# The first feed-forward product as seven half products, in a two-layer encoder kernel on one core

## The chip, the cores and the metric

The kernel runs on one core of a Trainium2 chip, as one program. The metric is the device time in microseconds (us) of one execution. Beside the times there is one execution recorded by the hardware profiler, from which all durations of single instructions come. The engines are called PE (TensorE, the matrix engine), DVE (VectorE), ACT (ScalarE), POOL (GpSimd) and SP (SyncE, which here only starts DMA transfers). A matmul first loads 128 columns of weights (PEld in the profile) and then streams the other operand through them.

## What is computed

A trunk of two layers over 512 positions of width 1024, all in float32. Each layer has an attention part of two head groups, then a feed-forward part of width 4096; the output gets a last norm. Cut to what matters here:

```python
for l in range(DEPTH):                       # 2
    h = rmsnorm(x, attn_norm[l])
    proj = jnp.einsum('bsd,de->bse', h, w_in[l])
    ...                                      # stick-breaking and differential attention
    x = x + jnp.einsum('bse,ed->bsd', mixed, w_o[l])
    h = rmsnorm(x, mlp_norm[l])
    u = jnp.square(jax.nn.relu(jnp.einsum('bsd,df->bsf', h, w_ff1[l])))   # 512 x 1024 by 1024 x 4096
    x = x + jnp.einsum('bsf,fd->bsd', u, w_ff2[l])                        # 512 x 4096 by 4096 x 1024
return rmsnorm(x, final_norm)
```

## The kernel before

**Precision.** Each float32 operand is split into two float32r parts: a high part, rounded by ACT (`activation` with `Copy` into a float32r tile), and a low part, the rest, taken by DVE. A product is then three matmuls into one PSUM sum: high by high, high by low, low by high (`three`, L257 to L262). For weights the split is `split_part` (L102 on; ACT at L117, DVE at L118), for other operands `split` (L218 to L220).

**Weights.** All weight blocks are units of 128 x 1024 in the order of their use (`_UNITS`). `_Weights.next` hands out the next unit and first has the units up to three behind it split (one behind it in the attention part, where there are two places instead of four). Units that aren't of kind "f" stream through a ring of three raw tiles, loaded by SP (L100). After a unit has been split, functions kept for it in `then` run: they start further loads.

**The feed-forward part** (from L754 on) goes through four groups of 1024 of the 4096 inner columns, `GROUPS`, in each layer. Per group:

- First product: eight blocks of 128 inner columns (`block`, called in the loop over `k`). A block is eight chunks of `three` with the unit's 128 x 128 weights and 512 positions of h streamed, into one PSUM bank; the banks turn among five. The rms factor of h isn't applied here but later, to y, since relu and square let it through as its square (`r2`). `evict_u` (L776 on) applies relu (L787) and square (L788) on ACT, and for each pair of blocks makes the four quarters and four combinations of u that Strassen's scheme wants, 256 positions wide, and splits them.
- Second product, already by Strassen's algorithm (in Winograd's form): seven forms (`FORMS`), each of two units, with u's combinations as weights and 512 columns of w_ff2 combinations streamed, into two PSUM banks. `gather` adds each form's banks to its own y tile: ACT copies at the first group (L810), DVE adds later (L812).

The combinations of w_ff2 are made by DMA: `fetch` loads a quadrant by SP (L754), and `grow` adds another onto it by an accumulating DMA from POOL (L760), as soon as the form that needs the earlier contents has been split: "11" grows into "x1", then "x2", then "x4", and "21" into "x3". Their tiles are `kept`.

In the last group the seven y tiles are merged (`merge`: accumulating DMA between tiles; `join`: DVE), scaled by `r2` (`settle`), transposed back onto x (`back`) or, in the last layer, normed and written out (`square`, `root`, `weigh`, `store`).

**Around it.** Before it stands the second half of the output projection, `wo(0)`, which per 128 rows of the model width makes h (`make_h`, L223 and L224) and the running sum of squares (`add_sq`; POOL adds, L233). PSUM has eight banks: two "t" for transposes, two "mm", three "s", one "o". The cosine and sine tiles are reloaded (or, in the last layer, replaced by the final gains) in group 1.

**What sets the order.** Each engine and each DMA queue works its instructions in one order, fixed when the program is built by a planner that follows the order of the text and its own estimates of readiness.

## Time and profile before

| what | value |
|---|---|
| runs | 1160.62, 1161.37, 1165.87 us; median 1161.37 |
| profiled execution | 1164.68 us, span from first to last instruction 1162.8 us |
| granted TensorE clock | 0.995 |
| ACT busy | 656.1 us (56%) |
| POOL busy | 174.7 us (15%) |
| read from HBM | 138.17 MB, written 2.10 MB |

How to read it: "xN" is a count; in a group's row stand line, engine, operation, output from inputs, shape, count, then busy us, mean ns of one, and the engine's idle time just before these instructions with what ended it. Consecutive instructions of one engine overlap a little in the rows, so the cost of one more is read from the distance of two starts.

### The profile page before, as it was taken

The page shows a single profiled execution, that of the slowest core. Times are in us where ns is not written, and L with a number is a line of the kernel's source. Part 1 is how long each engine was busy: PE and PEld are TensorE (multiplying, and loading weights), DVE is VectorE, ACT ScalarE, POOL GpSimd, SP SyncE. Part 2 cuts the span into 40 slices and gives each one's busy share as a digit, 9 for nine tenths or more (in the row PEclk, how much of TensorE's full clock was granted, in tenths as well). Part 3 has the DMA queues.
Part 4 walks back from the last instruction along what each step waited for, and adds up shares of the span by engine and source line. Part 5 has one row for each costly group of instructions (what it writes and reads, how often), then busy time and mean ns, then how long its engine had stood idle before and what let it go on. Part 6 is the DMA issues. An engine that isn't in the chain of part 4 may idle for free.

```text
span 1162.8 us, 15712 instructions
## 1 busy us (share of the span) xinstructions
PE 1142.8 (98%) x5682; PEld 961.8 (83%) x5682; DVE 799.1 (69%) x1291; ACT 656.1 (56%) x1169; POOL 174.7 (15%) x243
## 2 busy tenths in 40 slices
PE   9999999999999999999899999999999999999996
PEld 7889888888888888888688898888888888888884
DVE  6898688765546656656869976877664466476567
ACT  6456666566656455364445566655666553553554
POOL 1001423130101101002000024322211010010022
PEclk9999999999999999999899999999999999999998
DMA  7564443255945836737416733622658367376185
GB/s 255 172 179 130 128 134 102 73 216 112 215 145 113 224 115 130 231 89 160 97 55 183 218 109 109 181 67 72 228 125 218 125 129 222 93 176 190 29 172 131
DMA packets 56861, 170.13 MB, mean 146 GB/s; under 512 B 7120, under 2 KB 8144, under 8 KB 56784
## 3 DMA queue, kind: packets, MB, share of 16 engines
q1 hardware_dynamic: 46416, 131.88, 35.3%
q0 software_dynamic: 10224, 37.23, 18.7%
q8 instruction: 45, 0.74, 0.3%
q14 instruction: 32, 0.26, 0.1%
q10 hardware_dynamic: 144, 0.02, 0.0%
HBM read 138.17 MB, written 2.10 MB: 121 GB/s over the span
## 4 chain that ended last, share of the span: by engine, by line
PE 88%; DVE 5%; DMA 2%; ACT 2%; issue 1%; POOL 1%; POOLq 0%; ACTq 0%; DVEq 0%
PE f L260 10%; PE f L261 10%; PE f L262 10%; PE x L261 4%; PE x L262 4%; PE x L260 4%; PE wo L260 3%; PE wo L261 3%; PE wo L262 3%; DVE wlo L118 1%; PE T1s L533 1%; PE T0s L533 1%; DMA q<-in_w 1%; DMA y<-y 1%; PE v0w L260 1%
## 5 line engine op out<-in xcount | busy, mean ns | idle before, releaser
L118 DVE TENSOR_TENSOR wlo<-raw,whi 128x1024 fp32r<-128x1024 f32 (+1 forms) x132 | 157.5, 1197 | 101.6 <-ACT whi L117 101.2
L118 DVE TENSOR_TENSOR wlo<-q,whi 128x512 fp32r<-128x512 f32 x224 | 145.9, 687 | 109.2 <-ACT whi L117 108.8
L117 ACT ACTIVATE whi<-raw 128x1024 fp32r<-128x1024 f32 (+1 forms) x132 | 134.0, 1020 | 118.1 <-PE f L261 55.3
L260 PE MATMUL f<-h_hi,whi 128*128 128x512 f32 x512 | 199.6, 390 | 0.0
L262 PE MATMUL f<-h_hi,wlo 128*128 128x512 f32 x512 | 199.3, 389 | 0.0
L261 PE MATMUL f<-h_lo,whi 128*128 128x512 f32 x512 | 199.2, 389 | 0.0
L117 ACT ACTIVATE whi<-q 128x512 fp32r<-128x512 f32 x224 | 129.5, 624 | 121.5 <-DMA q<-in_w 39.7
L760 POOL DMA_DIRECT2D q<-in_w x64 | 56.2, 884 | 557.4 <-DVE wlo L118 470.7
L262 PEld LDWEIGHTS f<-h_hi,wlo 128*128 128x128 f32 x512 | 96.1, 188 | 20.0
L260 PEld LDWEIGHTS f<-h_hi,whi 128*128 128x128 f32 x512 | 96.1, 188 | 19.9
L261 PEld LDWEIGHTS f<-h_lo,whi 128*128 128x128 f32 x512 | 96.1, 188 | 19.8
L220 DVE TENSOR_TENSOR Al<-F,Ah 128x256 fp32r<-128x256 f32 (+2 forms) x96 | 74.8, 779 | 44.1 <-ACT Ah L219 44.0
L260 PE MATMUL x<-whi,Ah 128*128 128x512 f32 x256 | 100.6, 393 | 0.0
L261 PE MATMUL x<-wlo,Ah 128*128 128x512 f32 x256 | 100.2, 391 | 0.2 <-DVE wlo L118 0.2
L262 PE MATMUL x<-whi,Al 128*128 128x512 f32 x256 | 100.2, 391 | 0.0
L219 ACT ACTIVATE Ah<-F 128x256 fp32r<-128x256 f32 (+2 forms) x96 | 67.6, 704 | 45.7 <-DVE F L796 43.8
L261 PEld LDWEIGHTS x<-wlo,Ah 128*128 128x128 f32 x256 | 48.2, 188 | 10.3 <-DVE wlo L118 0.5
L260 PEld LDWEIGHTS x<-whi,Ah 128*128 128x128 f32 x256 | 48.2, 188 | 10.2 <-ACT whi L117 0.5
L262 PEld LDWEIGHTS x<-whi,Al 128*128 128x128 f32 x256 | 48.3, 189 | 10.0
L787 ACT ACTIVATE F<-f 128x512 f32<-128x512 f32 x64 | 37.5, 587 | 10.9 <-DVE Al L220 5.5
L788 ACT ACTIVATE F<-F 128x512 f32<-128x512 f32 x64 | 40.3, 630 | 1.5
L223 ACT ACTIVATE h_hi<-x,g_all 128x512 fp32r<-128x512 f32 x32 | 22.6, 720 | 26.0 <-DVE x L664 13.0
(920 smaller groups left out, 2600.2 us busy)
## 6 DMA issues: line engine op xcount, KB each, us to landing
raw<-in_w SPq DMA_DIRECT2D x126, 512.0 KB, 3.5
q<-in_w SPq DMA_DIRECT2D x64, 512.0 KB, 5.5
q<-in_w POOLq DMA_DIRECT2D x64, 512.0 KB, 6.1
x<-in_xT SPq DMA_DIRECT2D x8, 256.0 KB, 4.3
raw<-in_w SPq DMA_DIRECT2D x8, 128.0 KB, 4.2
yx<-y POOLq DMA_DIRECT2D x2, 512.0 KB, 8.5
y<-y POOLq DMA_DIRECT2D x2, 512.0 KB, 7.6
y<-yx POOLq DMA_DIRECT2D x2, 512.0 KB, 6.0
```

What stands on the lines that cost most here:

```text
L117: h = nc.scalar.activation(hi[:, a:b], raw[:, a:b], AF.Copy)
L118: self.last = h, nc.vector.tensor_tensor(out=lo[:, a:b], in0=raw[:, a:b], in1=hi[:, a:b].bitcast(F32), op=ALU.subtract)
L219: nc.scalar.activation(hi, src, AF.Copy)
L220: nc.vector.tensor_tensor(out=lo, in0=src, in1=hi.bitcast(F32), op=ALU.subtract)
L223: a = nc.scalar.activation(h_hi[:, c, :], x[:, c, :], AF.Copy, scale=g)
L260: nc.tensor.matmul(pt, ah, bh, start=first, stop=False)
L261: nc.tensor.matmul(pt, ah, bl, start=False, stop=False)
L262: nc.tensor.matmul(pt, al, bh, start=False, stop=last)
L533: nc.tensor.transpose(pt[:, n * P : (n + 1) * P], u["w"][qi][:, kb * P : (kb + 1) * P], ident)
L760: nc.gpsimd.dma_start(t, quad(g, q, c), accum_op=ALU.add)
L787: nc.scalar.activation(t, pt, AF.Relu)
L788: nc.scalar.activation(t, t, AF.Square)
```

## The change

The first product also goes by Strassen's algorithm. h, as 1024 model rows by 512 positions, is cut into four quarters (rows 0 to 511 and 512 to 1023; positions 0 to 255 and 256 to 511), w_ff1 of the group likewise into quadrants by model rows and by inner columns. Seven half products (`HALVES`), each of two units, stream 256 positions instead of 512. Their results aren't kept apart: "1", then "6", "7" and "4" add onto one PSUM sum (a); "5" and then "3" onto a second (b); "2" has a third (c). Between these additions `tap` reads the running sums out. There are two of each sum, one per unit of a half product, so six banks hold sums.

- The combinations of h (`T_hi`, `T_lo`) are made at the start of each layer's feed-forward part (`opening`): x is scaled into `hx` by ACT, combined by DVE and split, four pieces of 1024 columns.
- The combinations of w_ff1 are made from quadrants in the array `w1`: `fill` loads them (for "x" with an accumulating DMA on top), `sum1` adds two tiles by DVE and, for "y", starts another accumulating DMA. w_ff1 leaves the raw ring.
- u: `F` holds five slots of 128 x 1024 for a whole group. `roll` splits one slot, 1024 wide, two forms ahead of its use; two places turn. Three of the combinations are made after form "11".
- Units of the second product are split in one piece of 1024 instead of two of 512.
- The tile pools are moved: the attention's temporary tiles lie on the right side and are closed before `wo(0)`, so that loads of the first group are started ahead of `wo(0)`; the squares in `wo(0)` get two slots (the cosine and sine tile) instead of four; the cosines, sines, gains and the next layer's first raw units are loaded in the last group (`tables`).

```diff
+HALVES = ("1", "2", "5", "6", "7", "4", "3")
+FSLOT = {"11": 1, "21": 3, "x1": 4, "22": 3, "x2": 1, "x3": 0, "x4": 2}
...
-            for f in range(2 * GP):
-                units.append(("1", l, g * 2 * GP + f))
+            for q in HALVES:
+                for c in range(GP // 2):
+                    units.append(("q", l, g, q, c))
...
-            else:
-                self.split_part(i, 0, 512)
-                self.split_part(i, 512, 1024)
+            self.split_part(i, 0, 1024)
...
-                            add_sq(db, db == 0, tt)
+                            add_sq(db, db == 0, lambda n: cs[:, db % 2, :])
...
+            def fill(what, g, c):
+                t = homes[(what, c)] if what in "yw" else kept["z.x".index(what)][c]
+                for q in {"y": "1", "z": "2", "x": "5", "w": "4"}[what] + {"y": "7", "x": "63"}.get(what, ""):
+                    W.raw[_AT[("q", l, g, q, c)]] = t
+                nc.sync.dma_start(t, quad1(g, {"y": "11", "z": "12", "x": "21", "w": "22"}[what], c))
+                if what == "x":
+                    nc.gpsimd.dma_start(t, quad1(g, "22", c), accum_op=ALU.add)
+
+            def sum1(what, g, c):
+                i = _AT[("q", l, g, "5", c)]
+                t, by = W.raw[i], W.raw[_AT[("q", l, g, "1" if what == "y" else "2", c)]]
+                nc.vector.tensor_add(t, t, by)
+                if what == "y":
+                    nc.gpsimd.dma_start(by, quad1(g, "21", c), accum_op=ALU.add)
...
+                    then("q", g, "5", c, sum1, "y", g, c)
+                    then("q", g, "6", c, sum1, "z", g, c)
+                    then("q", g, "6", c, fetch, g, "11", c)
+                    if g == 0:
+                        then("q", g, "7", c, fetch, g, "21", c)
+                    then("q", g, "3", c, fetch, g, "22", c)
...
+                    if g + 1 < GROUPS:
+                        then("q", g, "7", c, fill, "y", g + 1, c)
+                        then("q", g, "4", c, fill, "w", g + 1, c)
+                        then("f", g, "22", c, fill, "x", g + 1, c)
+                        then("f", g, "x3", c, fetch, g + 1, "21", c)
+                        then("f", g, "x4", c, fill, "z", g + 1, c)
+                    elif c:
+                        then("q", g, "4", c, tables)
+            for what in "yzx":
                 for c in range(GP // 2):
-                    fetch(0, form, c)
+                    fill(what, 0, c)
+
+            for _ in wo(0):
+                pass
...
+            def opening(n):
+                if n == 0:
+                    scaled(range(4))
+                    nc.vector.tensor_sub(hx[:, top, hi_t], hx[:, top, hi_t], hx[:, top, lo_t])
+                    t_part(top, hi_t)
+                    scaled(range(4, 8))
+                elif n == 1:
+                    nc.vector.tensor_sub(hx[:, bot, hi_t], hx[:, bot, lo_t], hx[:, bot, hi_t])
+                    nc.vector.tensor_sub(hx[:, top, lo_t], hx[:, bot, lo_t], hx[:, top, lo_t])
...
+                    t_part(bot, lo_t)
+                elif n == 2:
+                    t_part(top, lo_t)
+                    nc.vector.tensor_add(hx[:, bot, hi_t], hx[:, bot, hi_t], hx[:, top, hi_t])
+                    t_part(bot, hi_t)
...
+                if q == "1":
+                    nc.scalar.copy(f(1), pt)
+                elif q == "2":
+                    nc.vector.tensor_add(f(1), f(1), pt)
+                    bend(1)
+                elif q == "6":
+                    nc.scalar.copy(f(0), pt)
+                elif q == "7":
+                    nc.scalar.copy(f(2), pt)
+                    nc.vector.tensor_add(f(2), f(2), sums[("b", c)])
+                    bend(2, -1.0)
+                elif q == "4":
+                    bend(3, -1.0, pt)
+                elif q == "3":
+                    nc.vector.tensor_add(f(0), f(0), pt)
+                    bend(0)
...
-                for k in range(2 * GP):
-                    for n, pt in enumerate(block(f"f{l}_{g}_{k}", "any")):
+                for q in HALVES:
+                    for c in range(GP // 2):
+                        if g == 0:
+                            opening(HALVES.index(q) * 2 + c)
+                        u = W.next("q")
...
+                        for i in range(2):
+                            for cc in range(4):
+                                three(pt[:, 256 * i : 256 * i + 256], wpair(u, 4 * i + cc), mover(q, cc),
+                                      q in "125" and i == cc == 0, i == 1 and cc == 3, q not in "125")
+                        tap(q, c, pt)
...
+                            if q == "2":
+                                roll("11")
+                            elif q == "4":
+                                roll("21")
+                            elif q == "3":
+                                nc.vector.tensor_sub(F[:, 4, :], F[:, 2, :], F[:, 0, :])
...
+                    if f + 2 < len(FORMS):
+                        roll(FORMS[f + 2])
+                    if f == 0:
+                        nc.vector.tensor_sub(F[:, 0, :], F[:, 1, :], F[:, 0, :])
+                        less(1, 4, 1)
+                        less(3, 1, 3)
```

`bend` is relu and square on ACT; `less` is one three-operand DVE instruction, 1024 wide; `mover` gives a quarter of h or of T.

202 lines of the change are left out of this document (112 added, 90 removed).

## The prediction

> **What bounds the kernel now.** I read the page's engine row first, then its chain that ended last, then the busy times of single stretches, then who waited for whom.
>
> ```profile
> PE 1142.8 (98%) x5682; PEld 961.8 (83%) x5682; DVE 799.1 (69%) x1291; ACT 656.1 (56%) x1169; POOL 174.7 (15%) x243
> ...
> PE 88%; DVE 5%; DMA 2%; ACT 2%; issue 1%; POOL 1%; POOLq 0%; ACTq 0%; DVEq 0%
> ```
>
> TensorE (PE) is busy 98% and holds 88% of the chain. A busy PE need not be a PE at its peak, so the next view takes two of the eight feed-forward groups (layer 0, groups 1 and 2), each cut between its first and its second product. The columns are us, then busy us of each engine, granted clock, DMA share and GB/s:
>
> ```profile
> core 0: us, PE busy (x) PEld busy (x) DVE busy (x) ACT busy (x) POOL busy (x), PEclk, DMA share, GB/s
> 325.10:368.60 43.50, 43.50 (x194) 36.03 (x193) 21.58 (x31) 24.52 (x37) 1.75 (x2) 1.00 0.42 114
> 368.60:406.70 38.10, 38.10 (x170) 31.56 (x169) 27.75 (x42) 18.25 (x29) 5.27 (x6) 1.00 0.82 204
> 406.70:450.20 43.50, 43.50 (x194) 36.03 (x193) 22.77 (x33) 23.46 (x35) 1.74 (x2) 1.00 0.42 111
> 450.20:488.30 38.10, 38.10 (x170) 31.56 (x169) 27.75 (x42) 18.25 (x29) 5.32 (x6) 1.00 0.82 206
> ```
>
> The reader is to see that PE fills every stretch at full clock; that VectorE (DVE) is the next busiest, 27.75 of 38.1 us in the second product; and that the DMA engines alternate between 0.42 and 0.82. In the view of waits from 243 to 572 us (the whole feed-forward part of layer 0) PE has only the last two of these rows (us in total, times, longest):
>
> ```profile
> DVE wlo L118 <- ACT whi L117: 104.1, 57, 7.5
> ...
> PE yT L849 <- DVE yx L843: 1.6, 1, 1.6
> ...
> PE x L261 <- DVE wlo L118: 0.2, 1, 0.2
> ```
>
> So PE alone sets the time there. The change is worth the PE time it takes out, less what the other engines then fail to hide.
>
> **The PE term.** First and last matmul of three unbroken runs in the order of time: 512 wide on f, 512 wide in the second product, and 256 wide in the values block, whose scheme (128 columns of weights loaded, 256 streamed, three matmuls a product) is that of the new half products:
>
> ```profile
> 259.67 0.39 PE L260 MATMUL f<-h_hi,whi 128*128 128x512 f32 x1
> ...
> 263.98 0.39 PE L261 MATMUL f<-h_lo,whi 128*128 128x512 f32 x1
> 475.23 0.39 PE L260 MATMUL x<-whi,Ah 128*128 128x512 f32 x1
> ...
> 479.99 0.39 PE L260 MATMUL x<-whi,Ah 128*128 128x512 f32 x1
> 605.47 0.28 PE L260 MATMUL v1w<-whi,h_hi 128*128 128x256 f32 x1
> ...
> 610.97 0.28 PE L261 MATMUL v1w<-wlo,h_hi 128*128 128x256 f32 x1
> L260 PEld LDWEIGHTS v0w<-whi,h_hi 128*128 128x128 f32 x64 | 12.2, 191 | 0.1
> ```
>
> The f run has 19 steps: 4.31/19 = 0.2268 us each. The x run has 21: 4.76/21 = 0.2267. The v run has 46: 5.50/46 = 0.1196. (The durations in the rows, 0.39 and 0.28, overlap; only the steps add up.) Twice 0.1196 exceeds 0.2268 by 0.012 us: a fixed cost per matmul, which halving the width pays twice.
>
> A group had 8 blocks x 8 chunks x 3 = 192 matmuls of 512: 43.55 us, as the 43.5 us stretches show. It gets 7 half products x 2 units x 2 x 4 x 3 = 336 of 256: 40.19 us. That is 3.36 us a group, 8 groups: **26.9 us less PE time**, where 7/8 of the multiplications alone would give 43.5. The second product keeps 168 of 512 (38.1 us), so a group goes from 81.6 to 78.3 us.
>
> The page "TensorE: Matmul & The Clock Gate" of the Trainium skill, section "Back-to-back issue gap", speaks against this change: it gives a sustained 131 ns a matmul at 512 columns and 81 at 128, so that a narrow matmul is far dearer per column. Between these, an estimate at 256 would be 98 ns, and 336 x 98 against 192 x 131 would add 7.8 us a group, 62 us in all. The trace disagrees, with 226.8 ns at 512 and 119.6 at 256. By that rule, slower; by the rows, faster.
>
> **DVE, and what shrinks its cover.** Prices, and how closely DVE instructions follow each other:
>
> ```profile
> L118 DVE TENSOR_TENSOR wlo<-raw,whi 128x1024 fp32r<-128x1024 f32 x124 | 154.5, 1248 | 101.6 <-ACT whi L117 101.2
> L118 DVE TENSOR_TENSOR wlo<-q,whi 128x512 fp32r<-128x512 f32 x224 | 145.9, 687 | 109.2 <-ACT whi L117 108.8
> L843 DVE SCALAR_TENSOR_TENSOR yx<-x,fin,yx 128x512 f32<-128x512 f32 x6 | 4.4, 742 | 0.0
> 442.12 0.68 DVE L793 TENSOR_TENSOR F<-F 128x512 f32<-128x512 f32 x1
> 442.72 0.69 DVE L220 TENSOR_TENSOR Al<-F,Ah 128x512 fp32r<-128x512 f32 x1
> ...
> 445.33 1.23 DVE L220 TENSOR_TENSOR Al<-F,Ah 128x1024 fp32r<-128x1024 f32 x1 [1.13 <-ACT Ah L219]
> 446.47 1.28 DVE L118 TENSOR_TENSOR wlo<-q,whi 128x512 fp32r<-128x512 f32 x2
> ```
>
> Back to back, 512 columns cost 0.60 us and 1024 cost 1.14; a three-operand one of 1024 about 1.3 (twice 0.66, from the 742 ns row less the same overlap). Per group, before to after:
> - low parts of weights: 8 x 1.14 + 28 x 0.60 = 25.9, to 28 x 1.14 = 31.9. The first product gets 14 units for 8; each second-product unit saves 0.06 by being split at once.
> - low parts of u: 4 x (0.35 + 0.60 + 1.14) = 8.4, to 7 x 1.14 = 8.0.
> - combinations of u: 4 x (0.60 + 2 x 0.35) = 5.2, to 2 x 1.14 + 2 x 1.3 = 4.9.
> - new: four sums of weights, 4.6, and six adds out of PSUM, 3.6.
> - adds to y: 14 x 0.60 = 8.4, unchanged.
>
> That is 47.9 to 61.4, +13.5. The rows show 50.5 (22.77 + 27.75) for the 47.9, so about 64 of 78.3 us: 82%, from 62%. It stays under PE. But five u splits and most combinations now fall in the second product: 14 x 1.14 + 5 x 1.14 + 3.7 + 8.4 = 33.8 us, and some 2 us of the last taps, in 38.1. DVE is in order and waits for ScalarE in every split, so it may fall a few us behind. Cover: a unit is split three units ahead (3 x 2.72 = 8.1 us, less 2.2 for its two halves: 5.9), and a roll of u has one form (5.44 us, less 2.2: 3.2). I price the remainder with the next term.
>
> **ScalarE.** Its rows:
>
> ```profile
> L117 ACT ACTIVATE whi<-raw 128x1024 fp32r<-128x1024 f32 x124 | 131.0, 1060 | 117.9 <-PE f L261 55.3 <-PE x L262 26.5 <-issue 6.4
> L787 ACT ACTIVATE F<-f 128x512 f32<-128x512 f32 x64 | 37.5, 587 | 10.9 <-DVE Al L220 5.5 <-PE f L262 5.4
> L788 ACT ACTIVATE F<-F 128x512 f32<-128x512 f32 x64 | 40.3, 630 | 1.5
> ```
>
> Per group: 28 weight halves and 7 rolls at 1.06, six PSUM copies at 0.59, eight relu and square pairs at 1.22: 50 of 78.3 us, 64%. The new waits are PE's: half product 7 may not go onto a sum until half product 6's copy has read it, and 4 not until 7's copy has. One unit of the other half (24 x 0.1196 = 2.87 us) lies between. Ahead of a copy stand at most a weight half and a pair, 1.06 + 1.22 + 0.59 = 2.87, just the cover. I take nothing, with up to 1 us a group at the bad end; behind a late copy wait the weight halves, which have 5.9 us.
>
> **DMA.** The page's queues, then issues over the run and in 362 to 400 us:
>
> ```profile
> q1 hardware_dynamic: 46416, 131.88, 35.3%
> q0 software_dynamic: 10224, 37.23, 18.7%
> ...
> q<-in_w POOLq DMA_DIRECT2D x64, 512.0 KB, 6.1
> ...
> q<-in_w POOLq DMA_DIRECT2D x6, 512.0 KB, 7.3
> L760 POOL DMA_DIRECT2D q<-in_w x64 | 56.2, 884 | 557.4 <-DVE wlo L118 470.7 <-DMA q<-in_w 81.4 <-issue 1.9
> ```
>
> Taken over the span of 1162.8 us, an accumulating half megabyte (0.524 MB) costs 0.187 x 1162.8 x 0.524/37.23 = 3.1 us of all sixteen engines, a plain one 0.353 x 1162.8 x 0.524/131.88 = 1.63. The plain count stays: 8 quadrant loads a group replace 8 raw loads. Accumulating ones go from 8 to 12 a group, two in each product. So the second product's 0.82 x 38.1 = 31.2 us of DMA become 37.4 of 38.1, the first's 18.3 become 24.5 of 40.2. The links at risk run in both kernels: split of 11, accumulate into x1, split, accumulate into x2, split, accumulate into x4, four units (10.9 us) apart. A link takes 0.9 issue + landing + 2.2 split, 10.4 us at 7.3 landing. What is added stands on POOL's queue: the accumulate for the next group's half product 5 waits for its own plain load on SP, and x4's stands behind it. x4's has 10.9 + 5.9 - 3.1 = 13.7 us for landing and that wait. Between 0 (all hidden, as the present PE rows) and 3.4 us a group (which returns the whole gain) I take, for DVE and DMA together and nearer the rows of now, 0.6: **+5 us**.
>
> **Start of each feed-forward part.** The last stretch before it:
>
> ```profile
> 221.00:243.50 22.50, 22.48 (x101) 18.28 (x100) 15.97 (x21) 12.90 (x20) 8.35 (x6) 1.00 0.30 94
> ```
>
> New there: eight scaled copies on ScalarE, five DVE combinations and four splits of T: 9 x about 1.15 = 10.5 us of DVE. Half products 1 and 2 need none of it, so PE runs 4 x 2.87 = 11.5 us before T is read and 17.2 before its second part. By 17.2 us DVE owes six weight halves 6.8, T 7, sums 2.3, taps and the norm's small reductions about 2.4: 18.5, against 17.2 and the 6.5 us that DVE has free in the stretch above, part of which takes earlier work. Bubbles between the two engines come on top. Bounds 0 and 6 us a layer; I take 3: **+6 us**. The loads for the first group move ahead of wo(0) onto SP, 6 x 1.63 + 2 x 3.1 = 16 us in a stretch with 0.7 x 22.5 = 15.8 free, and their last part is wanted only some 11 us after it: nothing. The squares get two slots for four; each gap of 2.7 us (eight in that stretch) holds them: nothing. The reload of cosines, gains and the next layer's first weights moves to the last group, some 40 us ahead of use: nothing.
>
> **Tails.** In the last group DVE feeds the merges and the way out; the rolls of x3 and x4 are new there, 2.3 us, against 0.06 a unit saved. Bounds 0 and 3 a layer, I take 1: **+2 us**.
>
> **Sum.** The profiled execution took 1164.7 us (span 1162.8): 1164.7 - 26.9 + 5 + 6 + 2 = 1150.8. It lies 3.3 above the median of the runs, 1161.4, so the forecast for the median is **1147.5**.
>
> **Rivals.**
> - *All hidden.* Every added piece finds cover: 1161.4 - 26.9 = 1134.5, with a tail or two 1137. For it: two PE rows now. Against it: the start is worked out as tight. Chance 0.10.
> - *DVE takes the second product.* 36 us of work with bubbles of 5 is 41 in 38.1, 3 a group: 24 in place of the 5, so 1166; with half of it 1157. For it: 104 us of DVE idle are waits for ScalarE. Against: most of that idle is lack of work. Chance 0.19, the time about as before.
> - *Slower: the accumulating loads become the chain.* With landing L, a link is L + 3.1 against 10.9; it decides from L = 7.8, and with the 5.9 us of lead over three links from 9.8. At L = 12 (four accumulates side by side are 12.4 us of all engines) a group loses 3 x 4.2 - 5.9 = 6.7, eight 54: 1147.5 - 5 + 54 = 1196. For it: 0.82 now, 7.3 where it is densest. Against: the gap it must close is 2.5 us. Chance 0.12.
> - *Narrow matmuls bound by the weight load.* If a load could not overlap, a step would be 0.191: 336 x 0.191 - 43.5 = 20.6 a group, 165 in all, 1326. The v rows show loads of 191 ns under steps of 119.6. Chance 0.01. (The rule of the Trainium skill quoted above would put its 62 us here.)
> - *The forecast*, 1141 to 1155: 0.58.
>
> Below half a per cent a run of this kernel can't be told from no change. Faster by more (under 1155.6): 0.68; within: 0.19; slower (over 1167.2): 0.13. The range leaves out half of "all hidden" and the two slower ones: 1137 to 1168.
>
> **What would show it.** First-product steps of 0.12 us in 40.2 us stretches, second ones of 38.1, prove the PE term. PE rows waiting for wlo or for Al name DVE; whi rows waiting for DMA, landings over 9.8, the chain; PE waits in the first 20 us on T the start. The forecast is wrong if PE's step in half products isn't 0.12, or if PE's waits in a middle group exceed 2 us.

## The result: slower, and the profile after

| kernel | runs | median us | profiled execution us | span us | clock |
|---|---|---|---|---|---|
| before | 4 | 1163.40 (1160.62 to 1165.87) | 1164.68 | 1162.8 | 0.995 |
| after | 4 | 1195.75 (1191.21 to 1199.01) | 1195.09 | 1193.3 | 0.983 |

The change makes the kernel slower by 2.8%: ratio 1.0276, 95% interval 1.0231 to 1.0321. The forecast was 1147.5, the range 1137 to 1168.

The page of the changed kernel: busy times, DMA queues, the two costliest groups on DVE and ACT, one of PE's groups of the second product, and the accumulating loads.

```profile
PE 1139.9 (96%) x6834; PEld 1002.5 (84%) x6834; DVE 922.2 (77%) x1221; ACT 718.5 (60%) x1137; POOL 201.4 (17%) x275
...
q1 hardware_dynamic: 46416, 131.88, 35.8%
q0 software_dynamic: 14832, 54.01, 25.5%
...
L123 DVE TENSOR_TENSOR wlo<-q,whi 128x1024 fp32r<-128x1024 f32 x184 | 224.6, 1230 | 128.9 <-ACT whi L122 128.5
L122 ACT ACTIVATE whi<-q 128x1024 fp32r<-128x1024 f32 x184 | 193.6, 1057 | 183.3 <-DMA q<-in_w 110.8
...
L262 PE MATMUL x<-whi,Ahx 128*128 128x512 f32 x256 | 105.0, 410 | 10.3 <-ACT whi L122 7.4
...
q<-in_w POOLq DMA_DIRECT2D x84, 512.0 KB, 7.0
```

The reader is to see three things. PE's busy time has fallen by 2.9 us only, although the forecast takes 26.9 out of it: its steps have become slower in places (behind waits the granted clock is lower, and some units step more slowly at full clock, both below), and slow steps count as busy. Plain loads move the same 131.88 MB as before, accumulating ones 54.01 instead of 37.23. And the rounding of weights by ACT now waits mostly for DMA: 110.8 of its 183.3 idle us. Before, the same rounding for the second product waited longer for PE (35.7 and 18.4) than for DMA (39.7):

```profile
L117 ACT ACTIVATE whi<-q 128x512 fp32r<-128x512 f32 x224 | 129.5, 624 | 121.5 <-DMA q<-in_w 39.7 <-PE f L261 35.7 <-PE x L262 18.4
```

The same two groups as in the prediction, cut in the same way (busy us by stretch):

```profile
core 0: us, PE busy (x) PEld busy (x) DVE busy (x) ACT busy (x) POOL busy (x), PEclk, DMA share, GB/s
337.60:377.60 40.00, 40.00 (x338) 39.99 (x337) 26.89 (x25) 27.86 (x38) 3.51 (x4) 1.00 0.62 147
377.60:419.70 42.10, 39.52 (x171) 31.33 (x169) 32.83 (x36) 20.20 (x21) 7.13 (x8) 1.00 0.87 209
419.70:459.70 40.00, 40.00 (x338) 40.00 (x337) 29.82 (x29) 27.28 (x36) 3.53 (x4) 1.00 0.60 149
459.70:503.70 44.00, 40.91 (x170) 32.32 (x170) 34.20 (x37) 20.20 (x21) 7.14 (x8) 0.97 0.85 202
```

The first products (first and third row) are down from 43.5 to 40.0 us with PE full, as forecast. The second products are up from 38.1 to 42.1 and 44.0, and PE stands still there for 2.6 and 3.1 us.

**Where the time went.** Cutting every group at the first matmul of its two products gives the whole difference of the spans, in us. The forecast's terms are put into the same slots (the last second products include the tails):

| slot | forecast | after less before | e9 (below) less before |
|---|---|---|---|
| first products of groups 1 to 3, six | -20.2 | -22.1 | -18.3 |
| first products of group 0, two (the starts) | -0.7 | +12.1 | -4.6 |
| second products of groups 0 to 2, six | +3.8 | +32.4 | +4.3 |
| last second products with the tails, two | +3.2 | +6.9 | +5.8 |
| the rest of the program | 0 | +1.2 | +1.2 |
| sum | -13.9 | +30.5 | -11.6 |

So there are two large losses: the second products, 5.4 us each, and the starts, 10 us each against the other first products. The experiments take them one by one. Where no range stands beside a time, the experiment is one execution. The four of the changed kernel lie up to 7.8 us apart, so that smaller differences are read from the stretches and not from the total.

### The profile page after: what moved, and what is told of

Read it like the earlier page. It is cut to its first block, busy times and chain, and to the rows that moved or that the text cites. A ratio compares the mean times of both kernels' runs of the same rounds, so it can differ in the third digit from the quotient of the medians.

```text
span 1193.3 us, 18142 instructions
## 1 busy us (share of the span) xinstructions
PE 1139.9 (96%) x6834; PEld 1002.5 (84%) x6834; DVE 922.2 (77%) x1221; ACT 718.5 (60%) x1137; POOL 201.4 (17%) x275
## 3 DMA queue, kind: packets, MB, share of 16 engines
q1 hardware_dynamic: 46416, 131.88, 35.8%
q0 software_dynamic: 14832, 54.01, 25.5%
## 5 line engine op out<-in xcount | busy, mean ns | idle before, releaser
L123 DVE TENSOR_TENSOR wlo<-q,whi 128x1024 fp32r<-128x1024 f32 x184 | 224.6, 1230 | 128.9 <-ACT whi L122 128.5
L122 ACT ACTIVATE whi<-q 128x1024 fp32r<-128x1024 f32 x184 | 193.6, 1057 | 183.3 <-DMA q<-in_w 110.8
L264 PE MATMUL f<-T_hi,wlo 128*128 128x256 f32 x512 | 146.1, 286 | 4.1 <-DVE wlo L123 4.1
L262 PE MATMUL f<-T_hi,whi 128*128 128x256 f32 x512 | 146.5, 286 | 1.5 <-ACT F L884 1.2
L263 PE MATMUL f<-T_lo,whi 128*128 128x256 f32 x512 | 146.2, 286 | 0.7 <-DVE T_lo L222 0.7
L262 PE MATMUL x<-whi,Ahx 128*128 128x512 f32 x256 | 105.0, 410 | 10.3 <-ACT whi L122 7.4
L775 POOL DMA_DIRECT2D q<-in_w x64 | 57.9, 936 | 315.6 <-DVE wlo L123 208.0
L264 PE MATMUL f<-h_hi,wlo 128*128 128x256 f32 x384 | 109.1, 284 | 2.1 <-DVE wlo L123 2.1
L262 PE MATMUL f<-h_hi,whi 128*128 128x256 f32 x384 | 109.3, 285 | 1.1 <-ACT whi L122 1.1
L263 PE MATMUL x<-wlo,Ahx 128*128 128x512 f32 x256 | 104.4, 408 | 6.2 <-DVE wlo L123 6.2
L263 PE MATMUL f<-h_lo,whi 128*128 128x256 f32 x384 | 108.9, 284 | 0.0
L262 PEld LDWEIGHTS x<-whi,Ahx 128*128 128x128 f32 x256 | 50.0, 195 | 24.4 <-ACT whi L122 9.8
```

Source lines behind the costliest of these rows:

```text
L122: h = nc.scalar.activation(hi[:, a:b], raw[:, a:b], AF.Copy)
L123: self.last = h, nc.vector.tensor_tensor(out=lo[:, a:b], in0=raw[:, a:b], in1=hi[:, a:b].bitcast(F32), op=ALU.subtract)
L262: nc.tensor.matmul(pt, ah, bh, start=first, stop=False, skip_group_check=onto)
L263: nc.tensor.matmul(pt, ah, bl, start=False, stop=False, skip_group_check=onto)
L264: nc.tensor.matmul(pt, al, bh, start=False, stop=last, skip_group_check=onto)
L775: nc.gpsimd.dma_start(t, quad(g, q, c), accum_op=ALU.add)
```

## Experiments on the second products

The theory: a group's weights for the second product grow in one tile from "11" over "x1" and "x2" to "x4", each step an accumulating load from POOL that waits for the split of what was there. The change puts two more accumulating loads into the same stretch, those of `fill("x")` for the next group, and they stand on POOL ahead of x4's, one before each. POOL's part of the timeline in group 1's second product after the change (start, us, then the instruction; in brackets the idle time before it and what ended it):

```profile
390.09 0.88 POOL L775 DMA_DIRECT2D q<-in_w  x1 [2.94 <-DVE wlo L123]
397.38 0.90 POOL L757 DMA_DIRECT2D q<-in_w  x1 [6.42 <-DMA q<-in_w]
398.01 1.18 POOL L775 DMA_DIRECT2D q<-in_w  x1
400.40 0.88 POOL L757 DMA_DIRECT2D q<-in_w  x1 [1.21 <-DMA q<-in_w]
403.72 0.88 POOL L775 DMA_DIRECT2D q<-in_w  x1 [2.44 <-DVE Y L920]
```

L757 is `fill("x")`, L775 is `grow`; the last two L775 rows are x4's two units. ACT rounds these units when they have landed, in the timeline of the same kernel:

```profile
407.04 1.06 ACT L122 ACTIVATE whi<-q 128x1024 fp32r<-128x1024 f32 x1 [3.81 <-DMA q<-in_w]
...
414.69 1.06 ACT L122 ACTIVATE whi<-q 128x1024 fp32r<-128x1024 f32 x1 [5.64 <-DMA q<-in_w]
```

The second unit was issued at 403.72 and rounded at 414.69: 11.0 us for a load whose median before was 7.3. The view of waits in 377.60 to 419.70 shows who pays (us in total, times, longest):

```profile
ACT whi L122 <- DMA q<-in_w: 16.2, 4, 5.6
...
POOL q L757 <- DMA q<-in_w: 7.6, 2, 6.4
...
PE x L262 <- ACT whi L122: 1.5, 1, 1.5
...
PE x L263 <- DVE wlo L123: 0.8, 1, 0.8
```

The rivals were that DVE is too full for the second product, and that the sheer volume of DMA is what costs.

**e1: `fill("x")` without its accumulating load**.

```diff
-                if what == "x":
-                    nc.gpsimd.dma_start(t, quad1(g, "22", c), accum_op=ALU.add)
```

> Left out: the accumulating load that adds quadrant 22 onto the weights of half product 5 (and so of 6 and 3). Two accumulating transfers fewer in each second product of groups 0 to 2. Theory A (the chain of accumulating loads sets the second product): landings there fall from 9.0 us towards 7, the second products of groups 0 to 2 from 41.4 to 45.2 us to under 40, six times some 4 us: about 1171. Theory B (DVE is too crowded there): the second products stay within 1 us, over 1188.

Measured: 1164.49 us, 31 below the change (the kernel before took 1164.26 beside it). All six second products of groups 0 to 2 take 38.70 us. Group 1's, in busy us:

```profile
370.70:409.40 38.70, 38.70 (x171) 31.52 (x170) 34.97 (x38) 20.55 (x21) 5.32 (x6) 1.00 0.83 202
```

DVE is busier than in the changed kernel, 34.97 of 38.70, and PE never waits for it. So DVE isn't the bound there. The starts stay at 49.4 and 49.7 us.

The two traces also show how x4's second unit comes late. Over the six groups it is issued 1.9 to 4.6 us later in the changed kernel than in e1, and it then lands after 9.7 to 10.9 us instead of 6.4 to 6.8. So both the place in the queue and the company of the other loads cost time, the company mostly a little more. The experiment doesn't yet tell order from volume, since it takes away both.

**e2: the same load triggered later in the text**, when x4 has been split instead of 22.

```diff
-                    then("f", g, "22", c, fill, "x", g + 1, c)
+                    then("f", g, "x4", c, fill, "x", g + 1, c)
```

> The same work, but the two-part load for the next group's half product 5 is started after the split of form x4 instead of form 22, so that on POOL's queue it stands behind the accumulates into x4 and falls into the first product. Theory A: second products of groups 0 to 2 lose 3 us or more each, about 1175, and the first products stay at 40.0. Theory B: no change, 1190 to 1200. If the volume alone counts, less than 1 us a group.

Measured: 1203.96 us, second products of 43.8 to 45.5. It tells nothing of the theory: the planner pulled the load forward to the old place on both queues, ahead of x4's (`fill` at 398.37 us, x4's first at 399.00 in group 1). A place in the text is not a place in a queue.

**e6: the order forced.** The accumulating load of `fill("x")` is tied behind both of x4's on POOL. The volume is that of the change, and in the trace the plain loads of `fill("x")` start where they did (12.8 us after the second product of group 1 begins, in both).

```diff
-                    nc.gpsimd.dma_start(t, quad1(g, "22", c), accum_op=ALU.add)
+                    a = nc.gpsimd.dma_start(t, quad1(g, "22", c), accum_op=ALU.add)
+                    if g:
+                        behind(a, grown["x4", 1])
...
-                nc.gpsimd.dma_start(t, quad(g, q, c), accum_op=ALU.add)
+                grown[form, c] = nc.gpsimd.dma_start(t, quad(g, q, c), accum_op=ALU.add)
...
-                        then("f", g, "22", c, fill, "x", g + 1, c)
+                        then("f", g, "x4", c, fill, "x", g + 1, c)
```

> The whole computation, the same transfers as the changed kernel, but on POOL's queue the accumulate for the next group's half product 5 is ordered behind both accumulates into x4 (the earlier try at moving it did not move it in the trace). If its place ahead of x4's accumulates is what costs (waiting for its own plain load and sharing the engines with them): second products of groups 0 to 2 lose 3 us or more, about 1175. If the volume of transfers costs wherever it lies: under 1 us a group, 1190 to 1200.

Measured: 1176.23 us, 19.5 below the change. Busy us by stretch in group 1, the second product and the first product after it:

```profile
370.90:409.60 38.70, 38.70 (x171) 31.51 (x170) 33.50 (x36) 19.40 (x20) 7.13 (x8) 1.00 0.92 216
409.60:451.40 41.80, 40.12 (x337) 39.94 (x336) 29.09 (x28) 28.22 (x37) 3.52 (x4) 1.00 0.61 153
```

POOL's part of the timeline (start, us; L779 is `grow`, L759 `fill`), and ACT's rounding of x4's second unit:

```profile
390.54 0.90 POOL L779 DMA_DIRECT2D q<-in_w  x1 [6.68 <-DMA q<-in_w]
395.33 0.88 POOL L779 DMA_DIRECT2D q<-in_w  x1 [3.89 <-DVE wlo L123]
395.87 2.14 POOL L759 DMA_DIRECT2D q<-in_w  x2
```

```profile
402.34 1.06 ACT L122 ACTIVATE whi<-q 128x1024 fp32r<-128x1024 f32 x1 [2.84 <-DMA q<-in_w]
```

The DMA share is higher than in the changed kernel, 0.92, and the second product has no stall: x4's second unit takes 7.0 us from issue to rounding (395.33 to 402.34) instead of 11.0, and is issued 24.4 us after the stretch began instead of 26.1. So in the second product not the volume but the order decides: five of them are 38.70 and one 39.52, together 27.9 us less than after the change. The volume isn't free, though. First products now take up to 43.5 us instead of 39.96, and 10.4 of the 27.9 us come back there. In the second row above PE stands still for 1.7 us, for a PSUM bank that DVE reads at L924. DVE works in order and first waits for the weights of half product 2, a plain load issued behind the accumulating ones, which lands after 10.4 us instead of 5.3 in e1. PE's wait in the view of waits of this stretch, then ACT's and DVE's rows in the timeline:

```profile
PE f L262 <- DVE Y L924: 1.7, 1, 1.7
```

```profile
411.21 1.06 ACT L122 ACTIVATE whi<-q 128x1024 fp32r<-128x1024 f32 x1 [5.87 <-DMA q<-in_w]
```

```profile
412.30 1.23 DVE L123 TENSOR_TENSOR wlo<-q,whi 128x1024 fp32r<-128x1024 f32 x1 [4.17 <-ACT whi L122]
413.44 1.28 DVE L924 TENSOR_TENSOR Y<-Y,x 128x512 f32<-128x512 f32 x2
```

**e5: no accumulating loads for the first product** from group 1 on. DVE adds the quadrants, 1.2 us an addition, in first products, where it has room. Full computation.

```diff
-                if what == "x":
+                if what == "x" and g == 0:
...
+                w = W.raw[_AT[("q", l, g, "4", c)]] if g else None
+                if what == "o":
+                    nc.vector.tensor_add(by, by, t)
+                    nc.vector.tensor_add(t, t, w)
+                    return
+                if what == "y" and g:
+                    nc.vector.tensor_add(t, by, w)
+                    return
...
+                    if g:
+                        then("q", g, "1", c, sum1, "o", g, c)
```

> The whole computation. From group 1 on the weights of half products 5, 6, 7 and 3 are summed by DVE from four loaded quadrants (four adds of 1024 a unit pair instead of two), and no accumulating load is left in the first product nor the two-part load in the second. Theory A: second products of groups 0 to 2 at 38.7 us as in the run without that load, first products still 40.0 (DVE 27 plus 4.6 of 40 us), starts still 50; 1163 to 1168. If DVE's 4.6 us more a group mattered, first products over 41.

Measured: 1167.79 us (1165.87 to 1173.72), 28 below the change; against the kernel before 1.0045, interval 1.0028 to 1.0062. All six second products are 38.70, five first products 39.96 and one 41.25, the starts still 51.1 and 50.1.

**e8: the mirror.** The kernel before, with nothing of the change, but one accumulating load more per unit, on the tile of the next group's 22: 12 more in all, as many as `fill("x")` has in the second products.

```diff
+                if g and form == "22":
+                    nc.gpsimd.dma_start(kept[k][c], quad(g, "21", c), accum_op=ALU.add)
```

> The kernel before, with one accumulating load more per unit pair: the next group's 22 quadrant gets another one added on top, as in the changed kernel's load for half product 5 (so its second product works on other weights). Theory A as the transfers alone: second products of groups 0 to 2 grow from 38.1 to over 41 here too, 20 us or more over the kernel before. If it takes a crowded DVE as well: under 1 us a group.

Measured: 1193.09 us against 1163.36 for the kernel before beside it, 29.7 slower. The six second products take 42.3, 45.0 and 44.4, then 39.8, 43.7 and 40.8 us instead of 38.08: 27.6 in all; the first products stay at 43.5 to 43.9, but for the one that takes 44.5 in the kernel before as well. The view of waits of one of them, 373 to 418 us:

```profile
POOL q L756 <- DMA q<-in_w: 9.8, 1, 9.8
...
PE x L260 <- ACT whi L117: 3.9, 1, 3.9
```

L756 is the added load. It waits on POOL for its plain load, as L757 does after the change, and x4's stand behind it. So a loss of nearly the same size (27.6 us against 32.4) is had without the half products and without their DVE work.

**e4: three combinations of u left out**, those behind form 11.

```diff
-                        nc.vector.tensor_sub(F[:, 0, :], F[:, 1, :], F[:, 0, :])
-                        less(1, 4, 1)
-                        less(3, 1, 3)
```

> Left out: the three combinations of u after form 11, 3.4 us of DVE in every second product. Theory B: each second product gets at least 3 us shorter, 24 in all, about 1171. Theory A: DVE waits for the landed weights anyway; under 1 us a group, 1187 to 1197.

Measured: 1185.27 us, 10 below the change, between what the two theories expected. Five of the six second products fall to 40.4 to 41.6, one stays at 44.8. The likely reason, argued from the rows of POOL above and not tested by itself: DVE's work is a part of each link, since the next load waits for DVE (2.94 and 2.44 us there), so less of it shortens the chain. A PE wait is left that e1, with the combinations, doesn't have.

## Experiments on the starts

In the changed kernel the first product of group 0 runs like this (layer 0, busy us):

```profile
244.70:262.00 17.30, 15.27 (x125) 14.66 (x124) 13.43 (x14) 14.52 (x21) 3.08 (x4) 1.00 0.17 43
262.00:270.00 8.00, 5.06 (x24) 4.46 (x23) 8.00 (x9) 4.30 (x6) 1.41 (x2) 0.70 0.42 66
```

From 262 to 270 us DVE is busy all the time, PE waits for it (0.73 us for the low part of T, then 1.89 for the low part of a weight), and the granted clock is 0.70: after the waits the matmuls follow each other in 0.21 instead of 0.12 us for some 6 us.

**e3: the opening left out** (half products 5, 6, 7 and 4 stream quarters of h itself).

```diff
-                a, b = ((h_hi, h_lo), (T_hi, T_lo))[which]
+                a, b = h_hi, h_lo
...
-                        if g == 0:
-                            opening(HALVES.index(q) * 2 + c)
```

> Left out: the combinations of h at the start (scaled copies, DVE combinations and their splits); half products 5, 6, 7 and 4 stream h instead. If the opening's work is what holds PE at the start, the first first-product of each layer goes from 50.0 us to 40 to 41 and the run to about 1175. If it is the first loads or the sum of squares on POOL, it stays over 46 and the run over 1187. Second products unchanged by either.

Measured: 1181.13 us, 14.6 below the change. The starts are 44.1 and 42.7 instead of 50.1 and 50.0, 13.3 in all. So the opening is the larger part, but 4.1 and 2.7 us are left against the other first products, which it doesn't explain. The second products still stall, 41.2 to 46.6.

**e7: the opening made early**, on e5: `hx` in a pool of its own, its combinations made row block by row block inside `wo(0)`, as x gets ready. The second unit of the first product also gets a free place.

```diff
+            def early(db):
+                nc.scalar.activation(hx[:, db, :], x[:, db, :], AF.Copy, scale=gcol("mlp", l, db))
+                if db == 3:
+                    nc.vector.tensor_sub(hx[:, top, hi_t], hx[:, top, hi_t], hx[:, top, lo_t])
+                    t_part(top, hi_t)
+                if db in (5, 7):
...
                             add_sq(db, db == 0, lambda n: cs[:, db % 2, :])
+                            early(db)
```

> The sums by DVE as in the run beside it, and the opening taken apart: h's scaled copies and combinations are made row block by row block inside wo(0), and the second unit of the first product gets a place that is free instead of the one of the last wo unit. If opening and that place are the start's loss: first first-products of 50.0 and 50.0 us go to 43 or less, 12 to 16 us from both layers against the run beside it: 1150 to 1154. If DVE is simply full from wo(0) on (52 of 51 us by prices): 47 to 49, the loss only moved into wo(0); 1159 or more.

Measured: 1169.34 us (1167.74 to 1170.89), no gain over e5; the starts are 50.7 and 50.8, even longer than the rival expected. DVE is busy without a break from about 236 us on, and its rows in the timeline show why:

```profile
236.31 0.75 DVE L226 SCALAR_TENSOR_TENSOR h_lo<-x,g_all,h_hi 128x512 fp32r<-128x512 f32 x1
236.97 2.32 DVE L839 TENSOR_TENSOR hx<-hx 128x1024 f32<-128x1024 f32 x1
...
242.07 1.78 DVE L226 SCALAR_TENSOR_TENSOR h_lo<-x,g_all,h_hi 128x512 fp32r<-128x512 f32 x1
```

POOL at the same times, adding the squares of x:

```profile
236.42 1.79 POOL L235 TENSOR_TENSOR ssq<-ssq,cs 128x512 f32<-128x512 f32 x1 [0.18 <-ACT cs L234]
...
241.67 1.64 POOL L235 TENSOR_TENSOR ssq<-ssq,cs 128x512 f32<-128x512 f32 x1 [2.62 <-ACT cs L234]
```

The same DVE instruction takes 0.75 us where it begins ahead of the addition (236.31 against 236.42) and 1.78 where the addition has begun before it (241.67 against 242.07). The one of 1024 begins during an addition that ends at 238.21, and itself ends 1.08 us after that: it took 2.32, and 1.22 in the next kernel, without POOL. The Trainium skill, "SBUF — State Buffer", section "Who interferes with whom", has the rule: VectorE's second input comes through a read port that it shares with GpSimd, and one of the two then waits for the other. The trace agrees, with these numbers. In layer 0 six such instructions of e7 are 6.0 us longer in all. The kernel before has the same seven additions and loses nothing on DVE: there `h_lo` each time begins 0.1 to 0.6 us ahead of the addition, as here:

```profile
240.35 0.75 DVE L224 SCALAR_TENSOR_TENSOR h_lo<-x,g_all,h_hi 128x512 fp32r<-128x512 f32 x1
```

```profile
240.46 1.79 POOL L233 TENSOR_TENSOR ssq<-ssq,sq 128x512 f32<-128x512 f32 x1 [1.48 <-ACT sq L232]
```

**e9: the squares moved.** On e7, the eight squares and their sums go into the first product of group 1, added by DVE, since only the last group's `settle` reads the result; the small reductions to `r2` move along. Full computation.

```diff
-                            add_sq(db, db == 0, lambda n: cs[:, db % 2, :])
...
-                        if (g, q, c) == (0, "2", 0):
+                        n_sq = HALVES.index(q) * 2 + c
+                        if g == 1 and n_sq < KC:
+                            add_sq(n_sq, n_sq == 0, lambda n: F[:, 4, 512 * (n_sq % 2) : 512 * (n_sq % 2) + 512], nc.vector)
+                        if (g, n_sq) == (1, 10):
```

> Full computation. The kernel e7_start_early with the eight squares of x and their seven sums on POOL (into ssq) taken out of the output projection ahead of the first product; they are done in the first product of group 1 instead, with the sums on VectorE, and the reciprocal mean square (rs_m, r2) moves there too, since only the last group's settle reads it. Theory (the starts are late because VectorE is full there, and about 8 us of that is POOL's seven additions, beside which VectorE's operations on two SBUF operands took 1.78 to 2.32 us instead of 0.68 to 1.21): the first product of group 0 goes from 50.7 to 42 to 45 us in each layer, the later ones stay near 40, and the run comes to 1153 to 1158, below the kernel before. Rival (VectorE is full there without POOL: opening, h_lo, x, weight splits): 48 to 51 us and 1165 to 1170, no change.

Measured: 1154.71 us (1153.0 to 1156.0), 14.6 below e7 and **faster than the kernel before: 0.9925, interval 0.9896 to 0.9954**. The starts are 41.8 and 41.6. The same cut of the first one (busy us by stretch), and the DVE row of `hx` from the timeline:

```profile
243.20:260.50 17.30, 16.67 (x140) 16.47 (x139) 17.30 (x21) 13.42 (x17) 1.76 (x2) 1.00 0.32 50
260.50:268.50 8.00, 7.24 (x61) 7.04 (x60) 6.75 (x7) 5.66 (x8) 0.00 (x0) 1.00 0.72 185
```

```profile
236.84 1.22 DVE L838 TENSOR_TENSOR hx<-hx 128x1024 f32<-128x1024 f32 x1
```

The rival, that DVE is too full there without POOL as well, falls: DVE is still full in the first 17.3 us, but PE now loses 0.6 us there, and the clock stays at 1.00. In layer 0 the start gets 8.9 us shorter. What e9 no longer has of e7 there is of that size: the 6.0 us on DVE, and two stretches of 3.4 us at half clock, each worth some 1.7 us of PE (an estimate from the granted clock). The move also frees ACT of the eight squares and DVE of the reductions there; no run takes these parts by themselves.

**e10: the same move alone**, on the changed kernel (its diff is that of e9).

> Full computation. The changed kernel itself, with that one move alone (squares and their sums out of the output projection into group 1). Theory: the opening's two row blocks and the weight splits of the first units run at their undisturbed times, and the start shortens from 50.0 by 3 to 6 us in each layer; the second products stay at 42 to 45 us, so the run comes to 1183 to 1190. Rival (the wait is on the opening's own chain hx, T_hi, T_lo): start within 1 us of 50.0, run 1193 to 1197.

Measured: 1190.56 us, 5 below the change, which is within the spread of the totals. The starts shorten by 2.6 and 3.6 us, to 47.4 and 46.4, in one layer less than expected; the second products still stall, 40.9 to 47.5. So neither the early opening (e7) nor the moved squares (e10) is enough by itself; together they take 17 of the 20 us.

## Experiments on what is left

**e11: the split u on the other side of SBUF**, on e9. In the changed kernel the matmuls of the second product step in two ways. First and last matmul of two units, twelve each, in group 2, from its timeline:

```profile
462.39 0.39 PE L262 MATMUL 11020_4829<-whi,Ah 128*128 128x512 f32 x1
...
464.88 0.39 PE L264 MATMUL 11021_4830<-whi,Al 128*128 128x512 f32 x1
465.11 0.40 PE L262 MATMUL 21020_4875<-whi,Ah 128*128 128x512 f32 x1
...
467.68 0.40 PE L264 MATMUL 21021_4876<-whi,Al 128*128 128x512 f32 x1
```

Eleven steps take 2.49 us in the one, 0.226 each, and 2.57 in the other, 0.234. With units of the slower kind the second product takes 38.70 us instead of 38.08, at full clock and without a wait (e1).

```diff
-                    rolls.append(right.enter_context(tc.tile_pool(name=f"ro{l}", bufs=2, side="right")))
+                    rolls.append(fctx.enter_context(tc.tile_pool(name=f"ro{l}", bufs=2)))
```

> Full computation. The kernel e9_squares_later with one change of place: the pool that holds the split u (Ah, Al, the stationary blocks of the second product) is taken from the side of SBUF on which the weight places 0 and 1 lie, as in the kernel before, instead of the side of places 2 and 3. Theory (a matmul of the second product steps in 0.2335 instead of 0.2267 us where the moving weights and the stationary u lie on different sides): units in places 0 and 1 then step in 0.2267, or the slow step moves to the units in places 2 and 3; in the first case the second products of groups 0 to 2 go from 38.8 to 38.1 and the run from 1154.7 to 1149 to 1151, in the second they stay at 38.8 with the slow units exchanged. Rival (the slow step has another cause, such as what else reads SBUF then): places 0 and 1 stay at 0.2335, no change of the time.

Measured: 1153.50 us (1151.26 to 1155.71), which can't be told from e9's; against the kernel before 0.9907, interval 0.9888 to 0.9925. Which units are slow has changed, but not as either theory said: steps of 0.227, 0.232 and 0.235 now stand side by side, and four of the six second products are 38.72 (the others 38.96 and 40.02). Moving one pool of tiles changed which units are slow, so the place of the tiles seems to have a part in it; what makes a step slow stays open.

**e12: the last layer's way out later**, on e11: two `settle`s two and four steps later in x2, two copies in x3.

```diff
-                        if end and form == "x2" and n in (1, 3):
-                            settle(2 + n // 2, 0)
+                        if end and form == "x2" and n in ((3, 7) if last else (1, 3)):
+                            settle(2 + n // (4 if last else 2), 0)
...
-                        if end and last and form == "x2" and n in (5, 6):
-                            nc.scalar.activation(place(n - 5, 1), turned(n - 5, 1), AF.Copy, scale=-1.0)
-                            if n == 6:
+                        if end and last and form == "x3" and n in (0, 2):
+                            nc.scalar.activation(place(n // 2, 1), turned(n // 2, 1), AF.Copy, scale=-1.0)
+                            if n == 2:
```

> Full computation. The kernel e11_u_beside with the last layer's settles of rows 2 and 3 two and four steps later in x2 and the two turned copies in x3. Theory (PE waits 4.5 us in the tail for the transposes' one bank, which VectorE frees only after the weights of x2 that came late): the gap of 4.5 us falls to under 2 and the last second product from 49.1 to 45 to 47, the run 2 to 4 us below e11_u_beside. Rival (the tail is bound by VectorE's own work behind the late weights, in whatever order): the last second product within 1 us of e11_u_beside's.

In the last second product of the changed kernel the view of waits has one long wait of PE, and e9 has the same:

```profile
PE xT L937 <- DVE Y L943: 4.1, 1, 4.1
```

Measured: 1152.94 us (1150.46 to 1155.31); against the kernel before 0.9906, interval 0.9888 to 0.9925. The last second product fell from 49.8 to 46.6 us in the profiled executions, and the wait's gap of 4.5 us between two matmuls to 1.95, with smaller ones beside it. The way out behind it got 1.5 us longer, so that 1.7 us are left of it to the end of the program. The times of e11 and e12 overlap, so not even these are shown in the whole.

## Why the prediction was wrong, by its own steps

- **The PE term** (26.9 us less) was right: a half-product group takes 39.96 us where 40.19 were forecast, and six groups gave 22.1 us for 20.2 (1 us of it from a first product that took 44.5 before). That narrow matmuls cost 0.12 us was right too: 338 in 40.00 us. That is against the rule of the Trainium skill that the prediction quotes ("TensorE: Matmul & The Clock Gate", section "Back-to-back issue gap").
- **DVE in the second product** was sized right (33.8 us and some taps forecast; 32.8 to 35.0 measured), and e1 shows that PE lives with it. The rival in which DVE takes the second product falls.
- **ScalarE** at nothing was right: PE's matmuls that may wait for ACT's copy out of PSUM lose 1.2 us of the whole run.
- **"+5" for DVE and DMA together is the step that failed.** The volume was right: 37.4 us of DMA forecast for a second product, 0.87 x 42.1 = 36.6 measured. The order on POOL was named too ("x4's stands behind it"). But the 13.7 us of room given to x4's load were not there. That figure took the whole lead of 5.9 us for the last link alone, though two links before it had used part. In e1, x4's second unit is issued 24.2 us after the second product begins and would be wanted in SBUF 33.2 us after it (38.1 less one unit of 2.72 and a split of 2.2): 9.0 us of room. Behind `fill("x")` the load took 11.0 and was issued 1.9 us later. That is 3.9 us late; PE stood still for 2.6 us of it, and the second product was 3.4 longer than in e1. Over six groups: 32.4 us, less 0.6 each for the slower steps, so 4.8 a group where 0.6 was taken. The prediction's own signs of being wrong came true: PE's waits in a middle group are over 2 us, and the landing of x4's second unit is over 9.8 in five of the six groups (9.7 in the other). That part of the lead was already in use could be read from the kernel before. There x4's second unit was issued 22.5 us after group 1's second product began at 369.15, which leaves 10.7 us and not 13.7:

```profile
391.65 0.88 POOL L760 DMA_DIRECT2D q<-in_w  x1 [5.46 <-DVE wlo L118]
```

- **The rival "the accumulating loads become the chain"** had the mechanism, and its time, 1196, is the measured 1195.75. The parts are not the same: it put 54 us on the chain and left 6 for the starts; measured are 29 and 20, so that the agreement of the sums is luck. It also counted eight second products, and only six have the added loads. Its chance of 0.12 was too low because the landing time was read from the queue of the kernel before (median 7.3) instead of from what two more loads ahead of it would make of it.
- **The starts** (3 us a layer, bounds 0 and 6) took 10. DVE's work was counted, 18.5 us owed in the first 17.2, but what that costs PE was put too low: without the opening (e3) the starts are 6.0 and 7.3 us shorter. The squares were given "nothing" for their two places, and there was no term for what POOL's additions take from DVE; without them there (e10) the starts are 2.6 and 3.6 shorter. And a gap on PE cost more than its length, since the clock halved behind it (0.50 from 266.4 to 270.0 us).
- **The tails** (1 us a layer) took 1.3 and 5.6 together with the last second products, of which about 0.6 each are slower steps. The 4.5 us gap in the last layer is PE waiting for a transpose's bank that DVE had yet to read.
- **Not foreseen** at all: the slower steps, about 5 us over the eight groups (an estimate: 8 x 0.62).

With the two failed steps mended, e9 takes 1154.7 where 1147.5 was forecast, just inside the forecast's own 1141 to 1155. That is partly luck, since e9 is another kernel than the one forecast. In the table it gains 11.6 us where 13.9 was forecast: the first products with their new sums and squares and the tails fall short, and the starts gain 3.9 more than forecast.

## What to carry to other kernels

Where a chain of loads feeds each other through an in-order queue, price a new load by what stands behind it on that queue and by the landing of the next link, not by its share of the bandwidth alone; and give the lead of a chain to all its links, once. Look for work on GpSimd beside a stretch in which VectorE becomes full: with two operands in SBUF, VectorE can pay for it, 6.0 us in e7 and nothing in the kernel before, where it began first each time. And where work is only needed much later, as the squares here, it need not stand where its input appears: a stretch with more room took it more cheaply.

## What the runs showed of the hardware that was not expected

- Two accumulating half megabytes more ahead of a load raised its time from issue to rounding from 7.0 us (e6) to 11.0 (the change), and the stretch with the shorter time has the higher share of the sixteen engines, 0.92 against 0.87.
- A gap of about 2 us on PE was enough for half the clock. In e7, PE waited 1.98 us once at the start of the first product, and in the stretch after that the granted clock was 0.54 (the timeline, then the busy us):

```profile
245.64 0.39 PE L264 MATMUL f<-h_hi,wlo 128*128 128x256 f32 x1 [1.98 <-DVE wlo L123]
```

```profile
245.60:249.00 3.40, 3.36 (x16) 3.36 (x17) 3.40 (x5) 3.40 (x6) 1.96 (x2) 0.54 0.00 0
```

  The Trainium skill, "TensorE: Matmul & The Clock Gate", section "Why this matters for your kernels", tells to leave no gaps over some 3 us; here the shorter one cost 3.4 us at half speed, and the measurement decides. No length of a gap that separates the cases came out of the runs: in e10 one of 1.89 us at 261.4 us left the clock at 1.00 until 266.4, and in layer 1 of the changed kernel gaps of 0.42 and 1.06 were followed by 3.4 us at 0.51.
- At full clock and without a wait, a 512-wide matmul steps in 0.227 us in some units and 0.234 in others; which units changed with the place of one pool of tiles (e11), and the cause stays open.
- In e7, a DVE instruction with two operands in SBUF that began during a POOL addition ended only 0.5 to 1.1 us after it. In the kernel before, where DVE began at least 0.1 us ahead all seven times, it kept its 0.75 us, and the addition took 1.79 us where it followed by 0.1 and 1.29 where by 0.6. That is no strict rule: in the changed kernel one `h_lo` with a lead of 0.14 us took 2.29.
